# Lower parts of weights and softplus moved from GpSimd to VectorE, and the second layer's state-space parameters issued later, in a two-layer hybrid block

## The chip, the cores and the metric

The kernel runs on one core of a Trainium2 chip. The metric is device time in microseconds of one execution, the median over runs. The engines are called by the names of the profile: PE (TensorE), DVE (VectorE), ACT (ScalarE), POOL (GpSimd), SP (SyncE, which issues the DMAs here).

## What is computed

Two layers, each an RMS norm, an input projection, three mixers side by side, an output projection, and a gated MLP. The sequence is 16 meta tokens and 512 tokens, width 1024, all in float32. Cut to the main lines:

```python
for l in range(2):
    hn = rmsnorm(h, norm1_g[l])
    sq, sk, sv, rq, rk, rv, rg, u = split(hn @ w_in[l])
    sb_o = stick_breaking(rmsnorm(sq), rmsnorm(sk), sv)      # 6 heads of 64
    ro = rmsnorm(retention(rotary(rmsnorm(rq)), rotary(rmsnorm(rk)), rv)) * silu(rg)   # 6 heads
    so = s5_mixer(u, lam, dt, B, C, d, w_glu)                # 16 groups of 16 channels, 64 states each
    h = h + concat(sb_o, ro, so) @ w_out[l]
    hn = rmsnorm(h, norm2_g[l])
    h = h + (silu(hn @ w_gate[l]) * (hn @ w_up[l])) @ w_down[l]
return h[:, 16:]

# stick_breaking, masked to s < t:
z = q @ k.T / 8
between = reverse_cumsum(log_sigmoid(-z)) - log_sigmoid(-z)
w = exp(log_sigmoid(z) + between);  out = w @ v
# s5_mixer, a complex linear recurrence per group g and state p:
x[l] = a * x[l-1] + (f*B) @ u[l];  y = Re(C @ x) + d*u;  y = gelu(y);  return y * sigmoid(y @ w_glu)
```

## The kernel before

Tiles hold 128 features by 528 positions (the 512 tokens of the last layer's end alone). A projection block is 128 output features; for each of 8 slices of the input width it takes three products, since every float32 operand is split into an upper and a lower part: xh by wh, xl by wh, xh by wl. Each product is two matmuls of 264 columns, so a block is 48 matmuls named pj. A weight arrives by DMA as wr, ACT copies it to the upper part wh, and `tensor_tensor` subtracts to give the lower part wl (`Unit.split`). `Unit.lo_eng` says on which engine: for the 23 projection blocks of a layer `WENG = (1, 1, 0)` gives two of three to POOL, of the output projection every second unit goes to POOL, and the MLP's all go to DVE. The attention's softplus is split in the same way: `sb_group` makes sp on DVE, hi on ACT, lo on POOL (`slow_split(s, n, G)`), and matmuls named z then add the running sums with the constant matrices tri and ones. Group widths are 432, 416 and 512 columns; there are 18 such splits in a layer, three head pairs by two heads by three groups.

The parameters of the state-space mixer are made by `s5_params` for each layer: `inputs(ri)` writes four pieces of ws and transposes them on PE (wps), `outputs` makes gg and bbd and multiplies them (kps), `phasors` doubles a table of rotations phr, phi from 1 to 132 columns with many small products (py, st). For the first layer they are shared by DVE and POOL. For the second they all run on POOL, beside the first layer's MLP, spawned at its second block.

The MLP goes through 22 blocks of 128 in parts of 8, 8 and 6. Of each block, gate and up are projected, DVE scales them out of PSUM (ga, up), ACT and DVE make the sigmoid si, POOL multiplies (up), DVE multiplies (ga), ACT makes hi, POOL lo. The eight down projections of a part come behind the gate and up of the next part's first block; they read hi and lo of all eight blocks, the eighth last.

The order of the work is set by a planner in the kernel. Every stage is a generator in `tasks`; between matmuls `tick` lets those go on whose time `t[1]` has come by a clock of estimated durations (`busy["PE"]`, with the costs in the `Timed` tables for V, SC and G). A task's time is raised by `spend` with each instruction and can be raised by hand (`now[0][1] += ...`). Behind it a scheduler of the framework orders the instructions once more, by its own estimates. Each engine then runs its queue strictly in order, so an instruction that stands ahead of its data holds back what is behind it.

Of the kernel before, what the change touches and what calls it, by code (L numbers as in the profile page):

```python
# [15 lines left out]
P = 128  # L16
# [4 lines left out]
KD = DM // P  # L21
DFF = 2816
NF = DFF // P
HALF = T // 2
NT_SLOTS = 62
AHEAD = 4
WLAG = 1000
LEAD = 200
# [4 lines left out]
ZBANKS = 4  # L33
GROUPS = 8
HOLD = (2, 0)
WENG = (1, 1, 0)
EPS = 1e-6
Q = 4
NCH = T // Q
# [46 lines left out]
COL = {"sq": C_SQ, "sk": C_SK, "sv": C_SV, "rq": C_RQ, "rk": C_RK, "rv": C_RV, "rg": C_RG, "u": C_U}  # L86
# [3 lines left out]
def hybrid_kernel(ctx, tc, A, out, dbg=None):  # L90
# [4 lines left out]
    now = [None]  # L95
# [35 lines left out]
    G = Timed(nc.gpsimd, "G", {"one": (180, 2.1), "two": (180, 2.1), "memset": (100, 0.85)})  # L131
# [53 lines left out]
    def banks(n):  # L185
        yield from take(n, "bank")
# [132 lines left out]
    plan, units = [], []  # L319
    for l in range(LAYERS):  # L320
        for i, (n, p) in enumerate(proj_order(l)):
            plan.append((A["w_in"][l, COL[n] // P + p], KD, P, G if plan and WENG[i % len(WENG)] else V))
        for ks in OUT_PARTS[l]:
            for m in range(KD // 2):
                plan.append((A["w_out"][l, m, :, ks[0]:ks[0] + len(ks), :], len(ks), 2 * P, G if m % 2 else V))
        for kind, i, f0, nf in mlp_order():
            if kind == "down":
                plan.append((A["w_down"][l, i, :, f0:f0 + nf, :], nf, P, V))
            else:
                plan.append((A["w_gate" if kind == "gate" else "w_up"][l, i], KD, P, V))  # L330
# [210 lines left out]
    def s5_params(l, engines, scal, par):  # L541
# [44 lines left out]
        def inputs(ri):  # L586

            mul, add, sub = on(engines[ri])
            pr, pi = powers(0, Q)
            x1, x2 = tt("btmp"), tt("btmp")  # L590
            ws = [tt("ws"), tt("ws")]
            for hf in range(2):
                G.memset(ws[hf], 0.0)
            mul(v4(x1, Q), wide(bbi if ri else bbr, Q), pr)
            mul(v4(x2, Q), wide(bbr if ri else bbi, Q), pi)
            yield
            for q in range(2):
                r = slice(64 * q, 64 * q + 64)
                for hf in range(2):
                    o = ws[hf][r, :512].rearrange("p (m c) -> p m c", c=32)[:, :, 16 * q:16 * q + 16]  # L600
                    a, b = (x[r, 256 * hf:256 * hf + 256].rearrange("p (m c) -> p m c", c=16) for x in (x1, x2))
                    (add if ri else sub)(o, a, b)
            yield
            for hf in range(2):
                yield from banks(1)
                ps = bank("wps")
                for t in range(4):
                    TE.transpose(ps[:, P * t:P * t + P], ws[hf][:, P * t:P * t + P], ident)
                yield
                we[ri, hf] = tt("we")  # L610
                SC.copy(out=we[ri, hf][:, :512], in_=ps)
                yield
                freed(1)
            over.append("inputs")

        def outputs():
# [21 lines left out]
            for ri, src in ((0, bbr), (1, bbi)):  # L638
                G.memset(bbd[ri][:, :256], 0.0)
                for q in range(2):  # L640
                    engines[ri].tensor_scalar(
                        out=bbd[ri][64 * q:64 * q + 64, :256].rearrange("p (t c) -> p t c", c=32)[:, :, 16 * q:16 * q + 16],
                        in0=src[64 * q:64 * q + 64], scalar1=-1.0 if ri else 1.0, scalar2=None, op0=ALU.mult)
            now[0][1] += 2000
            yield
            for hf in range(2):
                yield from banks(1)
# [186 lines left out]
    def sb_group(zp, g, gi, place, hl, ws):  # L834


        n = width(g)
        yield
        z = zp[:, :n]
        e = tt("e")  # L840
        SC.activation(e[:, :n], z, AF.Abs)
        SC.activation(e[:, :n], e[:, :n], AF.Exp, scale=-1.0)
        SC.activation(e[:, :n], e[:, :n], AF.Ln, bias=oneb)
        yield
        s = tt("sp")
        V.scalar_tensor_tensor(out=s[:, :n], in0=z, scalar=0.0, in1=e[:, :n], op0=ALU.max, op1=ALU.add)
        yield
        hl[gi] = yield from slow_split(s, n, G)

        for part in range(2):  # L850
            mm(zp[:, :n], lhsT=tri, rhs=hl[gi][part][:, :n], start=False, stop=True, more=True)
        behind = {}
        for j, q0, q1, o0 in g:
            for i, (g1, o1, p0) in place.items():
                if i > j:
                    a = max(q0, p0)
                    behind.setdefault(i, (g1, o1 + a - p0, q1 - a, []))[3].append(o0 + a - q0)
        if any(t[0] not in hl for t in behind.values()):
            yield lambda: all(t[0] in hl for t in behind.values())
        for g1, o1, w, to in behind.values():  # L860
            d, c = zp[:, to[0]:to[0] + w], slice(o1, o1 + w)
            if len(to) == 2:
                f = to[1] - to[0]
                d = zp[:, to[0] + w - f:to[0] + w + f].rearrange("p (t c) -> p t c", t=2)[:, :, f - w:]
            for part in range(2):
                x = hl[g1][part][:, c]
                mm(d, lhsT=ones, rhs=x[:, None, :].to_broadcast([P, 2, w]) if len(to) == 2 else x,
                   start=False, stop=True, more=True)
        yield
        SC.activation(e[:, :n], z, AF.Exp)  # L870
        yield
        freed(1, "scores", "bank")
        ws[gi] = e
# [442 lines left out]
```

## Time and profile before

| | us |
|---|---|
| median of 3 runs | 1374.18 (1373.87 to 1376.58) |
| the profiled execution, its time | 1374.02 |
| its span, first to last instruction | 1372.3 |
| PE busy | 1329.3 (97%) |
| DVE busy | 778.9 (57%) |
| ACT busy | 588.2 (43%) |
| POOL busy | 468.8 (34%) |

By stages: the first layer's projections, mixers and output projection run to about 312 us, its MLP to about 720, the second layer's mixers to about 970, its MLP to the end. A stretch in which PE is busy all the time is limited by the matmuls themselves. Where PE is not, what it waited for is named in the row behind it. The granted clock is that of TensorE as a share of 2.4 GHz.

### The profile page before, as it was taken

The numbers are of one execution on the slowest core, as the hardware profiler recorded it, in microseconds if no ns is written. First come the engines' busy times: TensorE is split into PE (matmuls) and PEld (weight loads), VectorE is DVE, ScalarE is ACT, GpSimd is POOL, SyncE is SP. The second block draws the span as 40 slices with busy tenths as digits, with TensorE's granted clock in tenths as the row PEclk, the third lists the DMA queues.
The fourth block names the chain that finished last, engine by engine and source line by source line (L and its number), as shares of the span: only waits on it lengthen the run. The fifth ranks groups of instructions, "written<-read, shape, count | busy, mean of one in ns | idle before, by whom it ended". The sixth has DMA issues, their size and how long they took to land.

```text
span 1372.3 us, 22298 instructions
## 1 busy us (share of the span) xinstructions
PE 1329.3 (97%) x9068; PEld 1212.8 (88%) x9068; DVE 778.9 (57%) x1261; ACT 588.2 (43%) x937; POOL 468.8 (34%) x598
## 2 busy tenths in 40 slices
PE   7989989999799999999999999999999999999998
PEld 6989879899799999999999899898788888888886
DVE  8874687767436345534567964334575543554453
ACT  5545545555233223322355466564354422332231
POOL 6593553322999012200233532342222210220120
PEclk9999999999999999999999999999999999999999
DMA  5212221222212322222222131312222322233223
GB/s 172 70 47 71 86 79 51 75 85 93 101 53 73 106 78 93 93 93 93 77 93 93 47 102 47 102 55 82 82 100 99 101 92 92 92 99 101 92 80 105
DMA packets 39127, 118.25 MB, mean 86 GB/s; under 512 B 4976, under 2 KB 5488, under 8 KB 39024
## 3 DMA queue, kind: packets, MB, share of 16 engines
q1 hardware_dynamic: 39024, 116.82, 26.0%
q8 instruction: 71, 1.16, 0.3%
q14 instruction: 32, 0.26, 0.1%
HBM read 111.46 MB, written 2.10 MB: 83 GB/s over the span
## 4 chain that ended last, share of the span: by engine, by line
PE 80%; DVE 10%; POOL 6%; ACT 2%; issue 1%; DMA 1%; SPq 0%; DVEq 0%; POOLq 0%
PE pj L138 70%; PE z L138 4%; PE hps L138 2%; PE av L138 1%; DVE fr L125 1%; PE ro L138 1%; DVE ysm L125 1%; DVE wl L125 1%; DVE fi L125 1%; POOL st L125 1%; DVE y L125 1%; POOL py L125 1%; POOL gg L125 1%; DVE s5w L125 1%; POOL ws L125 1%
## 5 line engine op out<-in xcount | busy, mean ns | idle before, releaser
L138 PE MATMUL pj<-xh,wh 128*128 128x264 f32 (+1 forms) x1792 | 448.2, 311 | 8.8 <-ACT wh L125 5.1
L138 PE MATMUL pj<-xh,wl 128*128 128x264 f32 (+1 forms) x1792 | 445.6, 309 | 1.4 <-DVE wl L125 1.4
L138 PE MATMUL pj<-xl,wh 128*128 128x264 f32 (+1 forms) x1792 | 445.1, 310 | 1.1 <-DVE xl L125 1.0
L125 ACT CAST wh<-wr 128x1024 fp32r<-128x1024 f32 (+3 forms) x210 | 206.2, 983 | 404.4 <-PE pj L138 372.4
L138 PEld LDWEIGHTS pj<-xh,wh 128*128 128x128 f32 x1792 | 296.5, 191 | 24.9 <-ACT wh L125 5.1
L138 PEld LDWEIGHTS pj<-xl,wh 128*128 128x128 f32 x1792 | 296.9, 190 | 18.7 <-DVE xl L125 1.6
L138 PEld LDWEIGHTS pj<-xh,wl 128*128 128x128 f32 x1792 | 295.8, 190 | 17.7 <-DVE wl L125 1.6
L125 DVE TENSOR_TENSOR wl<-wr,wh 128x1024 fp32r<-128x1024 f32 (+3 forms) x165 | 243.1, 1474 | 75.7 <-ACT wh L125 75.6
L138 PE MATMUL pj<-lo,wh 128*128 128x264 f32 (+1 forms) x720 | 192.9, 321 | 0.0
L138 PE MATMUL pj<-hi,wh 128*128 128x264 f32 (+1 forms) x720 | 192.2, 322 | 0.0
L138 PE MATMUL pj<-hi,wl 128*128 128x264 f32 (+1 forms) x720 | 191.9, 321 | 0.1
L125 POOL TENSOR_TENSOR up<-ga,up 128x528 f32<-128x528 f32 (+1 forms) x44 | 60.7, 1379 | 350.3 <-DVE up L125 350.3
L125 DVE TENSOR_TENSOR h<-h,pj 128x264 f32<-128x264 f32 (+1 forms) x144 | 69.3, 510 | 136.4 <-PE pj L138 136.1
L125 POOL TENSOR_TENSOR wl<-wr,wh 128x1024 fp32r<-128x1024 f32 (+3 forms) x45 | 95.9, 2133 | 148.2 <-ACT wh L125 126.4
L138 PEld LDWEIGHTS pj<-hi,wl 128*128 128x128 f32 x720 | 119.5, 188 | 10.9 <-DVE wl L125 0.5
L138 PEld LDWEIGHTS pj<-hi,wh 128*128 128x128 f32 x720 | 119.5, 188 | 10.8 <-ACT wh L125 0.6
L138 PEld LDWEIGHTS pj<-lo,wh 128*128 128x128 f32 x720 | 119.7, 188 | 10.0
L125 POOL TENSOR_TENSOR lo<-ga,hi 128x528 fp32r<-128x528 f32 (+1 forms) x44 | 59.0, 1341 | 156.4 <-ACT hi L125 156.3
L125 DVE TENSOR_TENSOR up<-pj,R 128x264 f32<-128x264 f32 (+1 forms) x66 | 32.1, 513 | 97.7 <-PE pj L138 97.7
L125 DVE TENSOR_TENSOR ga<-si,up 128x528 f32<-128x528 f32 (+1 forms) x44 | 31.8, 724 | 81.7 <-ACT si L125 58.4
L125 ACT ACTIVATE si<-si,bias 128x528 f32<-128x528 f32 (+1 forms) x44 | 32.1, 731 | 91.5 <-DVE si L125 91.5
L125 ACT ACTIVATE e<-z 128x432 f32<-128x432 f32 (+2 forms) x72 | 37.7, 547 | 44.7 <-PE z L138 44.3
(220 smaller groups left out, 1510.2 us busy)
## 6 DMA issues: line engine op xcount, KB each, us to landing
wr<-in_w_in_dram SPq DMA_DIRECT2D x44, 512.0 KB, 3.5
wr<-in_w_gate_dram SPq DMA_DIRECT2D x44, 512.0 KB, 3.5
wr<-in_w_up_dram SPq DMA_DIRECT2D x44, 512.0 KB, 3.5
wr<-in_w_down_dram SPq DMA_DIRECT2D x32, 512.0 KB, 3.5
wr<-in_w_out_dram SPq DMA_DIRECT2D x16, 384.0 KB, 3.2
wr<-in_w_down_dram SPq DMA_DIRECT2D x16, 384.0 KB, 3.1
rc<-in_rope_dram SPq DMA_DIRECT2D x12, 264.0 KB, 3.8
rs<-in_rope_dram SPq DMA_DIRECT2D x12, 264.0 KB, 3.9
```

The lines of the kernel that those rows point to most:

```text
L125: return f(*a, **k)
L138: nc.tensor.matmul(out, lhsT=lhsT, rhs=rhs, start=start, stop=stop, skip_group_check=more)
```

## The change

Three edits. The lower parts of all weights and of the attention's softplus are made on DVE (`WENG` is gone, G is V in two rows of the plan, and `slow_split(s, n)` takes its default engine); the split of the small matrix w_glu and the MLP's lo stay on POOL. The second layer's transposes are held back on the planner's clock by 12 us ahead of each half, and the products in `outputs` by 12 us in place of 2; for the first layer both numbers stay, with one more yield. The pool of 528-column tiles has 63 buffers in place of 62.

```diff
-NT_SLOTS = 62
+NT_SLOTS = 63
-WENG = (1, 1, 0)
         for i, (n, p) in enumerate(proj_order(l)):
-            plan.append((A["w_in"][l, COL[n] // P + p], KD, P, G if plan and WENG[i % len(WENG)] else V))
+            plan.append((A["w_in"][l, COL[n] // P + p], KD, P, V))
         for ks in OUT_PARTS[l]:
             for m in range(KD // 2):
-                plan.append((A["w_out"][l, m, :, ks[0]:ks[0] + len(ks), :], len(ks), 2 * P, G if m % 2 else V))
+                plan.append((A["w_out"][l, m, :, ks[0]:ks[0] + len(ks), :], len(ks), 2 * P, V))
...
             for hf in range(2):
+                now[0][1] += 12000 * l
+                yield
                 yield from banks(1)
                 ps = bank("wps")
...
-            now[0][1] += 2000
+            now[0][1] += 2000 + 10000 * l
             yield
...
-        hl[gi] = yield from slow_split(s, n, G)
+        hl[gi] = yield from slow_split(s, n)
```

What this does to the queues, at three places. On PE, in the first layer's MLP, at the end of the fifth block's gate projection (pj); wps are the transposes of the second layer's ws. Before:

```order
L138 MATMUL pj_4468<-xh_3838,wl_4322 128x264
L138 MATMUL pj_4469<-xh_3838,wl_4322 128x264
L144 MATMUL wps_4476<-ident,ws_4200 128x128 x4
L144 MATMUL wps_4504<-ident,ws_4201 128x128 x4
L144 MATMUL wps_4532<-ident,ws_4208 128x128 x4
L138 MATMUL pj_4545<-xh_3621,wh_4381 128x264
L138 MATMUL pj_4546<-xh_3621,wh_4381 128x264
```

And with the change, in the projections behind that place:

```order
L137 MATMUL pj_4613<-xh_3648,wh_4480 128x264
L137 MATMUL pj_4613<-xl_3649,wh_4480 128x264
L143 MATMUL wps_4624<-ident,ws_4200 128x128 x4
L137 MATMUL pj_4613<-xh_3648,wl_4481 128x264
L137 MATMUL pj_4613<-xh_3681,wh_4480 128x264
```

The first four transposes have 65 more pj matmuls ahead of them than before, and the three other groups follow 61, 48 and 26 pj matmuls apart, where three of the four stood together.

On POOL, in the same MLP, around lo of the eighth block (the row with ga and hi), which the first down projection reads; phr, phi, py and st are the phasors of the second layer. Before:

```order
L125 TENSOR_TENSOR phi_4227<-py_4228,py_4229 128x4x64
L125 TENSOR_TENSOR st_4241<-st_4241 128x4
L125 TENSOR_TENSOR phi_4236<-py_4237,py_4238 128x4x64
L125 TENSOR_TENSOR st_4232<-st_4232 128x4 x2
L125 TENSOR_TENSOR st_4241<-st_4241 128x4 x2
L125 TENSOR_TENSOR lo_5148<-ga_5134,hi_5147 128x528
L125 TENSOR_TENSOR py_4228<-phr_4226,st_4232 128x4x4
```

With the change:

```order
L124 TENSOR_TENSOR phi_4227<-py_4228,py_4229 128x4x32
L124 TENSOR_TENSOR st_4241<-st_4241 128x4
L124 TENSOR_TENSOR lo_5111<-ga_5097,hi_5110 128x528
L124 MEMSET tz_5161 128x528
L124 MEMSET tz_5283 128x528
L124 TENSOR_TENSOR phi_4236<-py_4237,py_4238 128x4x32
L124 TENSOR_TENSOR st_4232<-st_4232 128x4 x2
```

The doubling step on 64 columns stood ahead of this lo and now stands behind it, with the clearing of tz.

On DVE, in the first layer's attention, around the first softplus (sp) of the first head pair and the scaling of the second u block; wl are weights' lower parts, phr, phi, py, st the first layer's phasors. Before:

```order
L125 SCALAR_TENSOR_TENSOR sk_648<-sk_648,cols,hsq_763 128x528
L125 TENSOR_TENSOR u_891<-pj_723,R_143 128x264
L125 SCALAR_TENSOR_TENSOR sp_908<-z_753,e_833 128x416
L125 TENSOR_TENSOR u_891<-pj_724,R_143 128x264
L125 SCALAR_TENSOR_TENSOR sp_938<-z_754,e_837 128x416
L125 TENSOR_TENSOR py_803<-phr_801,st_807 128x4
L125 TENSOR_TENSOR py_804<-phi_802,st_807 128x4
L125 TENSOR_TENSOR phr_801<-py_803,py_804 128x4
```

With the change:

```order
L124 SCALAR_TENSOR_TENSOR sp_926<-z_760,e_791 128x416
L124 TENSOR_TENSOR lo_897<-sp_815,hi_896 128x432
L124 TENSOR_TENSOR u_965<-pj_888,R_143 128x264
L124 TENSOR_TENSOR py_851<-phr_849,st_855 128x4
L124 TENSOR_TENSOR u_965<-pj_889,R_143 128x264
L124 TENSOR_TENSOR py_852<-phi_850,st_855 128x4
L124 TENSOR_TENSOR wl_995<-wr_886,wh_994 128x1024
L124 TENSOR_TENSOR phr_849<-py_851,py_852 128x4
L124 TENSOR_TENSOR lo_1023<-sp_877,hi_1022 128x432
```

The lower parts of sp and of a weight now stand between the scaling of u and the phasors, in one queue with them.

## Rows read from the trace of the kernel before

**Rows 1.** The page: busy us (share of span) x instructions.
```profile
PE 1329.3 (97%) x9068; PEld 1212.8 (88%) x9068; DVE 778.9 (57%) x1261; ACT 588.2 (43%) x937; POOL 468.8 (34%) x598
```

**Rows 2.** Stretches: length, busy us by PE, PEld, DVE, ACT, POOL; granted clock, DMA.
```profile
48.00:100.00 52.00, 47.17 (x353) 43.92 (x352) 45.47 (x120) 27.56 (x52) 45.44 (x103) 0.97 0.15 52
140.00:200.00 60.00, 55.39 (x401) 48.98 (x401) 45.98 (x76) 28.76 (x55) 31.87 (x26) 0.97 0.26 85
368.00:383.00 15.00, 5.75 (x28) 5.14 (x28) 4.77 (x7) 3.70 (x5) 14.71 (x24) 0.66 0.10 37
383.00:440.00 57.00, 55.95 (x458) 54.94 (x457) 28.57 (x42) 20.34 (x29) 56.70 (x162) 1.00 0.20 66
440.00:720.00 280.00, 280.00 (x2296) 280.00 (x2296) 137.50 (x186) 94.20 (x121) 51.74 (x47) 1.00 0.28 91
740.00:800.00 60.00, 56.16 (x431) 52.59 (x431) 53.10 (x100) 29.94 (x54) 26.28 (x20) 0.97 0.21 71
```

**Rows 3.** Timeline of PE: start, us, what, xcount [idle before <-releaser].
```profile
368.06 0.40 PE L138 MATMUL pj<-xh,wl 128*128 128x264 f32 x2
376.65 1.97 PE L144 MATMUL wps<-ident,ws 128*128 128x128 f32 x8 [8.19 <-POOL ws L125]
...
380.45 0.79 PE L138 MATMUL pj<-xh,wh 128*128 128x264 f32 x2
...
383.64 0.60 PE L144 MATMUL wps<-ident,ws 128*128 128x128 f32 x4
```

**Rows 4.** Timeline of POOL at the same place.
```profile
373.93 6.39 POOL L125 TENSOR_TENSOR ws<-btmp,btmp 64x256 f32<-64x256 f32 x8
```

**Rows 5.** Who waited for whom, PE: us in total, times, longest.
```profile
PE pj L138 <- DVE u L125: 3.3, 1, 3.3
...
PE z L138 <- POOL lo L125: 1.5, 1, 1.5
...
PE kps L138 <- POOL bbd L125: 1.0, 2, 0.8
```

**Rows 6.** Groups by form: xcount | busy us, mean ns | idle before; the last from 460:480.
```profile
L125 POOL TENSOR_TENSOR wl<-wr,wh 128x1024 fp32r<-128x1024 f32 x30 | 72.5, 2419 | 96.6 <-ACT wh L125 91.6 <-ACT e L125 4.9
...
L125 POOL TENSOR_TENSOR lo<-sp,hi 128x512 fp32r<-128x512 f32 x12 | 17.6, 1480 | 19.7 <-ACT hi L125 11.0 <-issue 8.7
...
L125 DVE TENSOR_TENSOR wl<-wr,wh 128x1024 fp32r<-128x1024 f32 x3 | 3.7, 1225 | 0.6 <-ACT wh L125 0.6
```

**Rows 7.** Timelines of POOL and DVE, 24 to 32 and 68 to 74 us.
```profile
25.43 5.08 POOL L125 TENSOR_TENSOR wl<-wr,wh 128x1024 fp32r<-128x1024 f32 x2 [1.06 <-ACT wh L125]
...
28.30 2.33 DVE L125 TENSOR_TENSOR s5w<-s5p 128x16 f32<-128x16 f32 x2
...
30.76 0.70 DVE L125 TENSOR_TENSOR lo<-acc,hi 128x528 fp32r<-128x528 f32 x1
31.38 0.25 DVE L125 TENSOR_TENSOR s5w<-s5p 128x16 f32<-128x16 f32 x2
...
69.53 2.40 POOL L125 TENSOR_TENSOR wl<-wr,wh 128x1024 fp32r<-128x1024 f32 x1
...
69.71 2.24 DVE L125 TENSOR_TENSOR phr<-py,py 128x4 f32<-128x4 f32 x1
...
73.85 0.20 DVE L125 TENSOR_TENSOR phr<-py,py 128x8 f32<-128x8 f32 x1
```

**Rows 8.** POOL's busy us in the three dense stretches: tile wl, then tile sp.
```profile
sum 172.00, POOL 25.85; mean POOL 8.62
...
sum 172.00, POOL 15.79; mean POOL 5.26
```

**Rows 9.** POOL's and PE's timelines at the first down projection; a phasor group.
```profile
440.19 1.34 POOL L125 TENSOR_TENSOR lo<-ga,hi 128x528 fp32r<-128x528 f32 x1
...
445.16 0.40 PE L138 MATMUL pj<-hi,wh 128*128 128x264 f32 x2
...
L125 POOL TENSOR_TENSOR py<-phr,st 128x256 f32<-128x256 f32 x4 | 2.4, 611 | 0.0
```

## The prediction

> **What bounds the kernel now.** I read the page's share of busy time first, then the stretches, then the timeline where TensorE (PE) falls short. PE is busy 97% of the span [rows 1]. In the MLP of the first layer, from 440 to 720 us, it has no idle time at all: 2296 matmuls in 280 us, 0.122 us each, while VectorE (DVE) is busy half of the time and GpSimd (POOL) a fifth [rows 2]. Nothing done on DVE or POOL shortens such a stretch. Time can be won only where PE waits, and three kinds of places stand out: one hole at 368 to 383 us, where PE works 5.75 of 15 us at a mean granted clock of 0.66; and the attention stages of both layers, where PE loses a few us in each of the dense stretches 48 to 100, 140 to 200 and 740 to 800 us [rows 2]. In these three DVE is busy 45.5 of 52, 46.0 of 60 and 53.1 of 60 us, so it is the engine that PE comes to wait for there. The profiled execution took 1374.02 us (span 1372.3 and 1.7 around it); the median of the runs is 1374.18, so I sum against 1374.0 and take the result as the median's. A measurement of this kernel tells about 0.2% (2.7 us) from no change; "same" below means 1371.4 to 1376.9.
>
> **The change, part 1: the second layer's parameters are held back in the issue order.** In the kernel before, three rows of four transposes each (wps) stand in PE's queue directly behind the gate projection of the fifth MLP block. PE gets to them at 368.3 us and waits 8.19 us for POOL to write ws [rows 3]; POOL writes the eight pieces of ws in a row from 373.93 us on, 0.80 us each [rows 4]. PE does the queue in order, so ready matmuls stand behind. After the idle time PE is on the lower of its two clocks, 1.2 GHz: the first pair of pj matmuls takes 0.79 us in place of 0.41, and the mean of 0.66 in rows 2 says that the low level held for some 10 of the 15 us. The price: from 368.3 to 383.64 us, 15.3 us, PE does 12 transposes and 17 pj matmuls (nine rows, from the one at 380.45 on). At the pace of rows 2, 17 x 0.122 = 2.1 us; the transposes are at most 0.60 us for four, so 1.8 us, and less since such rows overlap the next. The loss is 15.3 - 2.1 - 1.8 = 11.4 us at least, about 12.0 with the overlap.
>
> In the new order the first four transposes stand 65 pj matmuls later, the next 61, 48 and 26 after that. At 0.122 us, PE gets to the first at 368.3 + 7.9 = 376.2 us, counted on the old clock of events. POOL's rows up to ws are the same in both orders, and POOL does not wait for PE there, so the third piece, the last one that the first transposes read, is there at 373.93 + 3 x 0.80 = 376.3. What is left of the wait is 0 to 0.5 us; the other three groups stand 3 us or more behind their data. **Minus 12.0 us**, and the half clock goes with it. Next late behind it are the kps matmuls, which wait 1.0 us for POOL's bbd [rows 5]. The change holds them back too (82 and 106 pj matmuls further), and in POOL's order bbd has moved ahead: **minus 1.0**. The new yield ahead of each transpose group and the added issue times are zero for the first layer; there only the planner's order moves.
>
> **Part 2: 81 lower parts go from POOL to DVE.** These are 45 of weights (30 with 1024 columns) and 36 of the attention's softplus (432, 416 and 512 columns). On POOL a weight's lower part takes 2419 ns, an attention one of 512 columns 1480; on DVE with POOL idle a weight's takes 1225 ns, and the same subtraction on 528 columns 0.70 us [rows 6, 7]. So DVE pays 0.51 of POOL's time for the one and about 0.46 for the other, an estimated 70 us in all (30 x 1.225 = 37; 15 smaller weights at about 0.8; 36 at 0.58 to 0.68), on a queue that lies beside PE's.
>
> What that costs or gives is not in those durations alone, and this is the unknown of the case. While POOL does a lower part, DVE's own instructions stretch. From 25.43 to 30.5 us POOL does two weights; in that time two DVE instructions on 16 columns take 2.33 us, and two of the same kind right after it 0.25. At 69.53 POOL starts another, of 2.40 us; DVE's phr<-py,py on 4 columns takes 2.24 us beside it, and 0.20 on twice the columns when POOL does short work [rows 7]. So DVE lost over 2 us to each, and would itself have needed 1.23. The Trainium skill ("SBUF — State Buffer", Who interferes with whom) states why: a DVE instruction with two SBUF inputs and a GpSimd instruction that reads SBUF hold a shared pair of ports for the whole instruction, and the second one blocks. The trace agrees at these places. Taken for every moved instruction, that rule would give back all of POOL's time below and make the time 1374.0 - 13.0 - 41.6 + 20.4 = 1339 at best.
>
> Two of PE's waits stem from this: the 3.3 us for u, whose read of PSUM stands behind that phr on DVE, and the 1.5 us for lo, which stands behind that weight on POOL [rows 5]. With POOL's part gone both causes are gone: **minus 4.8**, at most.
>
> Against it stands the longer DVE queue in the three dense stretches. The moved instructions fill 25.85 (weights) and 15.79 us (attention) of POOL's time there [rows 8]. On DVE they cost 25.85 x 0.51 + 15.79 x 0.46 = 20.4 us. What comes back is between nothing and all 41.6 us. The two places of rows 7 would give back over 80%, but both are instructions with two operands in SBUF, many of DVE's in the attention read PSUM (sp<-z, u<-pj), and where DVE waits for input nothing comes back; I take 40%, 16.6 us. The DVE queue is then 3.8 us longer in these stretches, and I charge it all to PE: **plus 3.8**. The ends are +20.4 and -21.2. Outside them I count nothing: DVE has idle time there, and from 440 to 720 us, where it is busy half of the time, PE never waits. [...]
>
> **Other moved work.** NT_SLOTS 63 adds one buffer to a pool of 62; I find no wait that names a missing tile, so nothing. The planner, given other costs, issues the attention's steps later against the pj matmuls (the last scores of the first layer's third pair stand behind its last projection, with no pj among them); part of the +3.8 is for that. The second layer's MLP stands in the same order in both.
>
> Sum: 1374.0 - 12.0 - 1.0 - 4.8 + 3.8 = **1360 us**.
>
> **Rivals.** *First, the attention wins more* (the blocked time comes back nearly whole): with 80%, 33.3 us, DVE's queue is 12.9 us shorter in the dense stretches. PE can win no more than it idles there, 4.8 + 4.6 + 3.8 = 13.2 us by rows 2, and 4.8 of it is counted. With half of the other 8.4: 1360 - 3.8 - 4.2 = 1352, down to 1348 with all of it. For it: rows 7. Against it: much of PE's waiting there is for chains (ScalarE's hsq, a rotation's DMA), not for DVE's load.
>
> *Second, DVE is a partial bound*: nothing comes back where it matters in one layer, half of the 20.4 is paid: 1360 - 3.8 + 10.2 = 1366, up to 1371. For it: DVE is 77 to 88% busy in those stretches.
>
> *Third, the hole moves.* POOL is busy 56.7 of 57 us from 383 to 440 [rows 2], with work that does not wait for PE, so without the hole PE comes 13 us earlier to whatever POOL makes. The first down projection reads the eighth block's lo 0.73 x 7 us after its start, at 445.16; POOL writes it from 440.19 to 441.5 [rows 9]. Had lo kept its place, PE would wait 441.5 - (445.2 - 13.0) = 9.3 us, and the time would be 1369. In the new order the whole last doubling of the phasors is behind lo: eight products of 0.61 us, 4.9 us, and an estimated 11 with their sums, the small steps between and the clearing of tz. So it lands at about 430.5, before 432.2; if only the 4.9 were saved it would come at 436.6 and PE would wait 4.4: 1364.
>
> *Fourth, slower than before*: DVE becomes what ends last in the dense stretches and gives nothing back; then PE pays the 20.4 whole and keeps the waits of 4.8: 1360 + 4.8 - 3.8 + 20.4 = 1381. It is slower than the bound if less than 4.5 of the 41.6 us comes back (20.4 - 4.5 = 15.9 against a gain of 13.0 plus 2.7). Rows 7 alone show more than 4 us of it.
>
> *Fifth, the change doesn't do what it says*: held back on the planner's clock, the transposes could still come before ws on the chip. The counts above say 0 to 0.5 us; if ws came 8 us later than I count, the first group would wait as before: about 1372.
>
> **How the numbers follow.** Forecast 1360 (1356 to 1364): 0.50. First rival 0.17, second 0.18, third 0.06, fourth 0.05, fifth 0.04. The range 1351 to 1370 takes in the forecast, most of the first rival, the second but for its end and the third: about 0.82. Faster (under 1371.4): 0.50 + 0.17 + 0.16 + 0.05 = 0.88; same: 0.02 + 0.01 + 0.04 = 0.07; slower: 0.05.
>
> **What would show it.** Part 1 is right if PE's wait for ws is under 1 us, the clock from 360 to 400 us is at 1.00 throughout, and the stretch between the two layers' attention is 13 us shorter. Part 2: POOL's busy time falls by some 140 us (both groups of rows 6 gone), DVE's rises by less than the 70 us that it pays; the difference is what came back. PE's waits for u (3.3) and for lo (1.5) should be gone; more waits for DVE in 140 to 200 us would be the second rival, a wait of the first down projection for lo the third. Wrong it would be if PE's idle time in the first 310 us grew by more than 13 us.

## The result, and the profile after

The changed kernel takes 1346.03 us (1345.35 to 1346.87), beside 1374.03 us (1373.74 to 1376.58) for the kernel before on the same chip: a ratio of 0.9787, with a 95% interval of 0.9775 to 0.9799. That is 28 us faster where I had forecast 14, and it lies below my range of 1351 to 1370. The profiled execution took 1346.14 us, its span is 1344.4. Of the run e7_none below, one of four executions took 3238 us at a granted clock of 0.40; its figures are those of the other three.

The busy times of the changed kernel, in the form of [rows 1]:

```profile
PE 1316.5 (98%) x9068; PEld 1203.5 (90%) x9068; DVE 800.6 (60%) x1342; ACT 586.8 (44%) x937; POOL 341.6 (25%) x517
```

POOL has lost 127 us, DVE has gained 22: the 81 moved instructions cost DVE some 70, so about 48 came back to it. On this my forecast was close. (The 81 took 142 us on POOL; the rest of POOL's work has grown by about 15, and why is not shown.) The same stretches as in [rows 2], of the changed kernel (length; busy us of PE, PEld, DVE, ACT, POOL; granted clock; DMA):

```profile
48.00:100.00 52.00, 51.49 (x414) 48.89 (x413) 48.80 (x136) 30.78 (x57) 47.85 (x115) 1.00 0.19 65
140.00:200.00 60.00, 56.21 (x439) 52.51 (x438) 48.68 (x89) 27.07 (x50) 18.62 (x18) 0.97 0.29 90
368.00:383.00 15.00, 13.99 (x114) 13.58 (x113) 8.02 (x13) 6.16 (x10) 14.92 (x45) 1.00 0.19 63
383.00:440.00 57.00, 57.00 (x468) 56.31 (x467) 29.32 (x44) 19.86 (x27) 55.60 (x140) 1.00 0.30 92
740.00:800.00 60.00, 58.45 (x463) 54.48 (x462) 50.54 (x87) 35.75 (x64) 9.60 (x7) 1.00 0.28 94
```

In two of the three dense stretches DVE is busier than before (48.8 against 45.5, 48.7 against 46.0), in the third less (50.5 against 53.1): 3.4 us more in all, near the 3.8 of my forecast. PE nevertheless does more in each: 414 matmuls against 353, 439 against 401, 463 against 431.

Stretches at fixed times hold different work in the two kernels. Two places can be found in every kernel of this case: the first matmul of the first layer's second norm (tile nps; the first layer's mixers and output projection are then done, and the first projections of the MLP, which do not need the norm yet, too, so this is later than the 312 us named above), and the same of the second layer's first norm (the first MLP is done). Cut there, each of the three stages holds the same work in both kernels: 2347 matmuls in the first, give or take one, 3175 in the second, 3552 in the third. The kernel before:

```profile
0.00:326.80 326.80, 304.30 (x2347) 283.61 (x2348) 239.66 (x524) 173.39 (x318) 158.02 (x231) 0.98 0.25 82
326.80:727.20 400.40, 390.10 (x3175) 388.48 (x3174) 195.12 (x266) 136.80 (x180) 152.17 (x257) 0.99 0.27 88
727.20:1372.00 644.80, 634.86 (x3552) 540.68 (x3550) 344.08 (x471) 278.04 (x441) 158.66 (x110) 1.00 0.27 87
```

and the changed one:

```profile
0.00:314.00 314.00, 296.53 (x2346) 279.34 (x2347) 246.85 (x565) 172.73 (x317) 98.46 (x190) 0.99 0.27 86
314.00:703.90 389.90, 387.46 (x3174) 386.18 (x3173) 193.79 (x268) 136.23 (x179) 150.64 (x255) 1.00 0.28 91
703.90:1344.00 640.10, 632.53 (x3552) 537.96 (x3550) 359.99 (x510) 277.86 (x441) 92.46 (x72) 1.00 0.27 88
```

So the 28 us are 12.8 in the first layer's mixers, 10.5 in its MLP and 4.6 behind it (645.1 to 640.5 up to the end of the spans). I had forecast 13 for the MLP and 1 for all the rest. In the first stage DVE is busy 7.2 us longer, and the stage is 12.8 us shorter. Of these 12.8 us, PE's idle time makes 5.0 (22.5 to 17.5) and its busy time 7.8 (304.3 to 296.5, for the same matmuls). The length of DVE's queue, by which I had priced it, points the wrong way.

### The profile page after: what moved, and what is told of

It is laid out like the page before. It is cut to its first block, busy times and chain, and to the rows that moved or that the text cites. A ratio compares the mean times of both kernels' runs of the same rounds, so it can differ in the third digit from the quotient of the medians.

```text
span 1344.4 us, 22300 instructions
## 1 busy us (share of the span) xinstructions
PE 1316.5 (98%) x9068; PEld 1203.5 (90%) x9068; DVE 800.6 (60%) x1342; ACT 586.8 (44%) x937; POOL 341.6 (25%) x517
## 4 chain that ended last, share of the span: by engine, by line
PE 87%; DVE 6%; POOL 3%; ACT 2%; issue 1%; DMA 1%; SPq 0%; DVEq 0%; POOLq 0%; ACTq 0%
PE pj L137 75%; PE z L137 4%; PE hps L137 2%; PE av L137 1%; PE ro L137 1%; DVE wl L124 1%; ACT e L124 1%; DVE ysm L124 1%; POOL gg L124 1%; PE kps L137 1%; POOL ws L124 1%; PE rtp L143 0%; ACT uc L124 0%; POOL btmp L124 0%; PE kv L137 0%
## 5 line engine op out<-in xcount | busy, mean ns | idle before, releaser
L137 PE MATMUL pj<-xh,wh 128*128 128x264 f32 (+1 forms) x1792 | 454.4, 310 | 15.2 <-ACT wh L124 4.9
L137 PE MATMUL pj<-xl,wh 128*128 128x264 f32 (+1 forms) x1792 | 454.8, 310 | 1.2 <-DVE xl L124 1.2
L137 PE MATMUL pj<-xh,wl 128*128 128x264 f32 (+1 forms) x1792 | 452.4, 309 | 0.3 <-DVE wl L124 0.3
L124 DVE TENSOR_TENSOR wl<-wr,wh 128x1024 fp32r<-128x1024 f32 (+3 forms) x210 | 292.9, 1395 | 84.9 <-ACT wh L124 82.1
L137 PEld LDWEIGHTS pj<-lo,wh 128*128 128x128 f32 x720 | 119.9, 188 | 10.1
L124 ACT CAST hi<-ga 128x528 fp32r<-128x528 f32 (+1 forms) x44 | 27.6, 627 | 62.2 <-DVE ga L124 62.2
```

The lines of the kernel that those rows point to most:

```text
L124: return f(*a, **k)
L137: nc.tensor.matmul(out, lhsT=lhsT, rhs=rhs, start=start, stop=stop, skip_group_check=more)
```

## Experiments

Three questions: is the MLP's gain that of the holds; is the mixers' gain that of the engine (DVE no longer blocked, lower parts no longer late) or that of the planner's new order; and what does a us of work on DVE cost PE, against a us in which POOL blocks DVE? The stage times (the same cuts, from the trace of one execution of each run; the last to the end of the span) and the ratios, which are over all executions:

| kernel | lower parts made on | plan | holds | mixers 1 | MLP 1 | the rest | ratio to before (95%) |
|---|---|---|---|---|---|---|---|
| before | POOL | POOL's costs | no | 326.8 | 400.4 | 645.1 | 1 |
| changed | DVE | DVE's costs | yes | 314.0 | 389.9 | 640.5 | 0.979 (0.978 to 0.980) |
| e1_holds | POOL | POOL's | yes | 330.0 | 388.9 | 652.8 | 0.997 (0.996 to 0.998) |
| e2_engines | DVE | DVE's | no | 315.3 | 400.2 | 639.8 | 0.986 (0.984 to 0.988) |
| e5_plan | POOL | DVE's | yes | 324.1 | 389.4 | 641.7 | 0.987 (0.985 to 0.988) |
| e6_queue | DVE | POOL's | yes | 315.1 | 389.1 | 646.6 | 0.983 (0.982 to 0.985) |
| e7_none | nobody | POOL's | yes | 304.7 | 394.0 | 640.7 | 0.974 (0.972 to 0.975) |
| e8_unread | POOL, not read | POOL's | yes | 325.6 | 389.0 | 645.4 | 0.991 (0.989 to 0.993) |
| e3_sp_pool | softplus's on POOL | DVE's | yes | 316.7 | 389.5 | 645.8 | 0.983 (0.982 to 0.985) |
| e4_wl_pool | weights' on POOL | DVE's | yes | 321.0 | 389.2 | 643.9 | 0.986 (0.985 to 0.988) |
| e9_yield | POOL | POOL's | yield only | 329.2 | 398.3 | 649.5 | 1.005 (1.003 to 1.007) |
| e11_lead | DVE | DVE's, LEAD 220 | yes | 312.9 | 390.2 | 642.7 | 0.981 (0.979 to 0.984) |
| e12_lead_before | POOL | POOL's, LEAD 220 | no | 324.6 | 398.9 | 646.4 | 0.997 (0.996 to 0.998) |
| e10_more | DVE, and 18 more | DVE's | yes | 319.9 | 389.5 | 641.3 | 0.983 (0.981 to 0.986) |

The profiled execution need not be the median one: of e9_yield it took 1378.8 us and the median is 1382.1, of e11_lead 1347.5 and 1349.3. So differences of a few us between single stages are to be read with care. The kernels whose lower parts POOL makes by POOL's plan, and the two that leave them out, have 62 of the 528-column buffers, all others 63; this third edit was not varied by itself.

### One part alone

The kernel before with the holds:

```diff
+                now[0][1] += 12000 * l
+                yield
                 yield from banks(1)
                 ps = bank("wps")
...
-            now[0][1] += 2000
+            now[0][1] += 2000 + 10000 * l
```

> The kernel before with part 1 alone: the second layer's transposes and the products of outputs are held back by 12 and 10 us, all lower parts stay on POOL. My forecast gave this part -13.0 us of its sum, so 1361 us, with the hole at 368 to 383 us gone. If the parts add up and the attention is where the rest of the gain lies, the change's total of 28 us leaves 15 to 20 us for part 2, so part 1 alone is 1361 to 1364 us. If the hole is not the holds' doing (rival: POOL, freed of the weights' lower parts, is simply earlier with ws), part 1 alone gives less than 6 us: 1368 us or more.

It took 1372.28 us, where the kernel before took 1375.94 on that chip: 0.3% faster. By its time that is the rival's range (1368 or more), but the stages tell otherwise. The MLP is 11.5 us shorter, as my forecast has it, while the first layer's mixers are 3.2 us longer and the rest 7.7. So the holds close the hole by themselves, with POOL as busy as before, and most of the gain is lost elsewhere; what takes it is the question of e9_yield below.

The other part alone is the changed kernel with both edits of the diff above undone:

> The changed kernel without the holds: the 81 lower parts are on DVE, the second layer's transposes stand where the planner then puts them. By my forecast's sum part 2 alone is worth -1 us: 1373. If the parts add up with what was measured for both (1346) and part 1 is worth 10 to 13, it is 1356 to 1359 us. If POOL's relief alone closes the hole, it is 1350 us or less.

It took 1357.2 us, a gain of 1.4% and as expected if the parts add up (1356 to 1359), and the MLP is as long as before (400.2). PE waits there for POOL just as in [rows 3]; of what PE waited for (us in total, times, longest):

```profile
PE wps L143 <- POOL ws L124: 9.3, 2, 8.2
```

So POOL's relief does not close the hole, the holds do, and part 2 is worth 18.7 us alone, where my sum had 1. On the changed kernel the holds are worth 10.3 us in the MLP and about the same in the time (the ratios are 0.9861 and 0.9787, which is 10.2 us), since the mixers lose nothing there.

### Engine or order

The planner decides the order by the costs of the engine that it is told. So the two can be taken apart: `X` is issued on one engine and spends the other's costs.

```diff
+    X = Timed(nc.gpsimd, "V", {"one": (150, 1.05), "two": (160, 1.2)})
...
-            plan.append((A["w_in"][l, COL[n] // P + p], KD, P, V))
+            plan.append((A["w_in"][l, COL[n] // P + p], KD, P, X if plan and WENG[i % len(WENG)] else V))
...
-        hl[gi] = yield from slow_split(s, n)
+        hl[gi] = yield from slow_split(s, n, X)
```

> The changed kernel's plan with the engine of before: the planner is told DVE's costs for the 81 lower parts, so that PE's order is nearly that of the changed kernel, but the instructions are issued on POOL. Theory A (the gain in the attention is the new order of the work): it keeps most of the attention's gain, 1346 to 1351 us. Theory B (the gain is that DVE and the chains behind the lower parts no longer stand behind POOL's slow instructions): most of that gain goes, 1357 us or more, and worse than that where the plan now expects a lower part earlier than POOL has it.

The mirror image starts from the kernel before with the holds, with `X = Timed(nc.vector, "G", {"one": (180, 2.1), "two": (180, 2.1)})` in G's place.

> The other way round, holds included: the planner is told POOL's costs for the 81 lower parts, so that PE's order is nearly that of the kernel before with the holds alone, but the instructions are issued on DVE. Theory A (order): little of the attention's gain is left, 1356 to 1361 us. Theory B (blocked DVE instructions and slow chains): most of it is there, 1346 to 1351 us. If DVE's longer queue cost what my forecast charged (3.8 us) and only the waits for u and lo went, 1359 to 1361 us.

They took 1357.8 us (theory B) and 1353.1 us (between the two), and the stages sort it. In the first layer's mixers the engine counts: 330.0 to 315.1 in the old order, 324.1 to 314.0 in the new one, while the order makes 5.9 with POOL and 1.1 with DVE. Behind the MLP it looks like the order: 652.8 to 641.7 and 646.6 to 640.5, while the engine makes 6.2 in the old order and 1.2 in the new one. The first pair differs in the number of buffers too; the second (both 63) does not, and gives the engine 10.1 us in the mixers. The orders of a pair are near each other but not the same. Written by name and shape in the order of the trace, PE's 9,068 matmuls of e5_plan differ from the changed kernel's in 402 lines, from those of the kernel before in 2,278; those of e6_queue differ from e1_holds in 452.

### What blocking costs, and what the work costs

These two leave the lower parts out of the result. In the first nobody makes them, in the second POOL makes them and no matmul reads them; in both the matmuls read zeros in their place, as many as before.

```diff
+            if self.lo_eng is X:
+                b = zero[:, None, :self.c].to_broadcast([P, self.kt, self.c])
...
-        return R_(a), R_(b)
+        return R_(a), zero if lo_eng is X else R_(b)
```

> The kernel before with the holds, planned with POOL's costs, but the 81 lower parts are left out on every engine: nobody makes them, and the matmuls that would read them read a tile of zeros (the same number of matmuls; the lower parts' share of the result is missing). It shows what these lower parts cost in all where POOL does them, and, against the same plan with them on DVE (1353 us), what DVE's longer queue costs PE. By my forecast's sum DVE's 20.4 us in the dense stretches are paid by PE: 1353 - 20 = 1333 us. If DVE's queue is not what PE pays for: 1349 to 1353 us.

> As the run that leaves the lower parts out, and with PE's order the same as there, but POOL makes all 81 lower parts as before, into tiles that no matmul reads (the matmuls read zeros, so the lower parts' share of the result is missing). POOL's work is there, and nobody waits for its results. Theory B1 (POOL's instructions block DVE's): it is 10 to 18 us slower than the run without them, so 1360 us or more. Theory B2 (PE waits for lower parts that are late on POOL): it is within 3 us of that run, and the whole difference to the holds alone (1372) is PE's waiting.

They took 1338.3 us, between the two values given for it, and 1362.25 us: 24.0 us apart (20.6 between the profiled executions), with PE's order the same but for 26 lines. No matmul waits for what POOL makes in the second, so the difference is what POOL's presence does to others. That is theory B1, and more than its 10 to 18 us. What is left to the holds alone (ratios 0.9911 and 0.9969, 8 us) is what waiting for late lower parts can have cost at most, as far as the two can be compared: their orders differ in 942 lines, and PE's list of waits there has 1.5 us for a lower part on POOL. The groups of DVE's instructions show how POOL acts on them. With nobody making the lower parts (xcount | busy us, mean ns | idle before):

```profile
L125 DVE TENSOR_TENSOR wl<-wr,wh 128x1024 fp32r<-128x1024 f32 (+3 forms) x165 | 250.0, 1516 | 75.9 <-ACT wh L125 75.6
...
L125 DVE TENSOR_TENSOR h<-h,pj 128x264 f32<-128x264 f32 (+1 forms) x144 | 69.5, 510 | 137.9 <-PE pj L143 137.5
...
L125 DVE SCALAR_TENSOR_TENSOR sp<-z,e 128x432 f32<-128x432 f32 (+2 forms) x36 | 21.9, 622 | 18.4 <-ACT e L125 14.6 <-PE pj L143 3.8
...
L125 DVE COPY uc<-u 32x132 f32<-32x132 f32 x32 | 8.9, 278 | 0.5
...
L125 DVE SCALAR_TENSOR_TENSOR sq<-sq,cols,hsq 128x528 f32<-128x528 f32 x6 | 5.5, 924 | 4.2 <-ACT hsq L125 4.2
...
L125 DVE SCALAR_TENSOR_TENSOR rk<-rk,cols,hsq 128x528 f32<-128x528 f32 x6 | 4.7, 780 | 5.4 <-ACT hsq L125 5.4
...
L125 DVE TENSOR_SCALAR s5w<-s5w 128x16 f32<-128x16 f32 x13 | 2.4, 215 | 0.0
```

and with POOL making them unread:

```profile
L125 DVE TENSOR_TENSOR wl<-wr,wh 128x1024 fp32r<-128x1024 f32 (+3 forms) x165 | 245.7, 1489 | 73.9 <-ACT wh L125 73.8
...
L125 DVE TENSOR_TENSOR h<-h,pj 128x264 f32<-128x264 f32 (+1 forms) x144 | 69.6, 510 | 138.1 <-PE pj L139 137.7
...
L125 DVE SCALAR_TENSOR_TENSOR sp<-z,e 128x432 f32<-128x432 f32 (+2 forms) x36 | 21.8, 622 | 16.3 <-ACT e L125 12.4 <-PE pj L139 3.8
...
L125 DVE COPY uc<-u 32x132 f32<-32x132 f32 x32 | 11.0, 343 | 0.5
...
L125 DVE SCALAR_TENSOR_TENSOR rk<-rk,cols,hsq 128x528 f32<-128x528 f32 x6 | 8.8, 1473 | 5.0 <-ACT hsq L125 4.9
L125 DVE SCALAR_TENSOR_TENSOR sq<-sq,cols,hsq 128x528 f32<-128x528 f32 x6 | 8.6, 1425 | 8.6 <-ACT hsq L125 8.6
...
L125 DVE TENSOR_SCALAR s5w<-s5w 128x16 f32<-128x16 f32 x13 | 4.7, 385 | 0.0
```

What has an operand in PSUM beside one in SBUF (h, whose pj is in PSUM; sp, whose z is) takes the same 510 and 622 ns. Several groups of the mixers that read two operands in SBUF take longer beside POOL, such as rk with 1473 ns in place of 780 and sq with 1425 in place of 924. Not every such group does: DVE's own wl, most of it in the MLPs, where POOL does the same work in both runs, takes 1489 and 1516 ns. Two kinds with one operand in SBUF take longer too, the COPY (343, 278) and the TENSOR_SCALAR (385, 215). In each of these it is one instruction, held behind a weight on POOL; for the COPY (two of them in the first row, one of the usual length):

```profile
724.62 2.64 DVE L125 COPY uc<-u 32x132 f32<-32x132 f32 x2
...
724.74 2.39 POOL L125 TENSOR_TENSOR wl<-wr,wh 128x1024 fp32r<-128x1024 f32 x1 [6.57 <-ACT wh L125]
```

All of DVE's work is 779.3 us against 737.3, the same 1262 instructions; ACT's is 587.5 us in both, and PE's commonest matmul (pj with xh and wh) takes 311 ns against 309 in the mean.

One place shows how that reaches PE. With POOL at work, DVE (above), POOL and PE (the last row), start and us:

```profile
68.94 2.26 DVE L125 TENSOR_TENSOR phr<-py,py 128x4 f32<-128x4 f32 x1
71.23 1.03 DVE L125 TENSOR_TENSOR py<-phr,st 128x4 f32<-128x4 f32 x1
...
74.70 2.32 DVE L125 TENSOR_TENSOR py<-phi,st 128x16 f32<-128x16 f32 x1
...
77.89 0.43 DVE L125 TENSOR_TENSOR u<-pj,R 128x264 f32<-128x264 f32 x1
...
68.77 2.41 POOL L125 TENSOR_TENSOR wl<-wr,wh 128x1024 fp32r<-128x1024 f32 x1
71.13 1.11 POOL L125 TENSOR_TENSOR lo<-sp,hi 128x432 fp32r<-128x432 f32 x1
...
74.65 2.34 POOL L125 TENSOR_TENSOR wl<-wr,wh 128x1024 fp32r<-128x1024 f32 x1
...
78.37 0.59 PE L139 MATMUL pj<-xh,wh 128*128 128x264 f32 x1 [6.86 <-DVE u L125]
```

and the same DVE instructions where POOL doesn't make them:

```profile
63.12 0.17 DVE L125 TENSOR_TENSOR phr<-py,py 128x4 f32<-128x4 f32 x1
63.33 0.17 DVE L125 TENSOR_TENSOR py<-phr,st 128x4 f32<-128x4 f32 x1
...
65.92 0.20 DVE L125 TENSOR_TENSOR py<-phi,st 128x16 f32<-128x16 f32 x1
...
67.08 0.42 DVE L125 TENSOR_TENSOR u<-pj,R 128x264 f32<-128x264 f32 x1
```

Three instructions on 4 to 16 columns take 5.6 us in place of 0.5, and each ends within 0.03 us of POOL's instruction beside it (71.20 and 71.18, 72.26 and 72.24, 77.02 and 76.99). Behind them stands the reading of u out of PSUM, 9.0 us after the first of them in place of 4.0, and behind that PE, which waits 6.86 us.

Now the two prices. The first stage of three kernels in the old order: nobody, POOL unread, DVE (e6_queue).

```profile
0.00:304.70 304.70, 295.30 (x2346) 278.75 (x2347) 212.29 (x525) 173.72 (x317) 92.15 (x191) 1.00 0.28 88
```

```profile
0.00:325.60 325.60, 301.82 (x2347) 283.53 (x2348) 238.88 (x525) 173.77 (x318) 158.60 (x232) 0.98 0.26 83
```

```profile
0.00:315.10 315.10, 299.36 (x2346) 279.74 (x2347) 248.45 (x565) 174.13 (x317) 95.62 (x190) 1.00 0.27 86
```

With POOL at work DVE is busy 26.6 us longer by blocking alone (40% of POOL's 66.5), and the stage is 20.9 us longer: 0.79 us for each us. With the work on DVE it is busy 36.2 us longer, and the stage 10.4: 0.29 for each. Behind the MLP there is no such difference in the old order: POOL costs 4.7 us, DVE 5.9. All in all POOL's presence costs 24.0 us for 42.0 us more of DVE's busy time (0.57 for each), DVE's work 13.5 (by the ratios, 0.9736 and 0.9834) for 67.6 more (804.9 against 737.3; 0.20 for each). Three things blur the figures of DVE's work: e6_queue's order differs from the other two in some 930 lines, it has one buffer more, and without any lower parts the MLP is 5 us longer, 2.9 of them one wait for a weight's lower part at 420 us.

### Which of the lower parts

The changed kernel and its plan, with only the softplus's or only the weights' lower parts issued on POOL, by the same `X`:

> The changed kernel with its plan (DVE's costs for all 81), but the 36 lower parts of the softplus are issued on POOL; the weights' stay on DVE. With all 81 on POOL in this plan it was 1357.8, so there are some 12 us to divide. If POOL blocks DVE in proportion to its time, the softplus has 47 of 143 us: 1350 us. If what counts is that the matmuls behind the softplus wait longer for its lower part, most of the 12 us is here: 1354 us or more.

> The changed kernel with its plan, but the 45 weights' lower parts are issued on POOL as in the kernel before; the softplus's stay on DVE. In proportion to POOL's time (96 of 143 us) it loses 8 of the 12 us: 1354 us. If the matmuls behind the softplus are what counts: 1346 to 1349 us.

They took 1352.89 and 1356.51 us. In the first layer's mixers the softplus costs 2.7 us there, the weights 7.0, all together 10.1 (e5_plan): a sum of 9.7, in the shares 28 and 72%, close to the 33 and 67% of POOL's time. No sign, then, that the matmuls behind the softplus count for more. In the whole time neither meets its proportion (1350 and 1354): the two add to 17 us and both at once cost 11.8; the difference lies behind the MLP (645.8 and 643.9 against 641.7), where I can't tell it from reordering.

### How much a reordering makes

> The kernel before with only the added yield ahead of each transpose group (no hold, all lower parts on POOL). With the holds alone the stretch of the first layer's MLP became 11.5 us shorter, but the time fell by less than 4: the first layer's mixers ended 3 us later and the second layer's took 4 us more. If the yield's reordering of the first layer's mixers is what took the 3 us: the first layer's mixers end at 329 to 331 us here too (327 in the kernel before) and the time is 1376 to 1380. If the loss belongs to the holds, which act in the second layer only, the mixers end as before and the time is 1374 to 1376.

The yield alone took 1382.12 us, 0.5% slower, a little above the 1376 to 1380 that I gave for its theory. The first layer's mixers end at 329.2 us, as with the holds (330.0). PE's waits show the same new places in both, such as 5.1 us for u where it was 3.3 in [rows 5] and 3.7 for y that the kernel before didn't have:

```profile
PE pj L138 <- DVE u L125: 5.1, 1, 5.1
PE pj L138 <- DVE y L125: 3.7, 1, 3.7
```

So the yield, which does nothing but reorder, explains the 3 us in the mixers, and 4.4 of the 7.7 us behind the MLP; the other 3.3 are not explained.

> The changed kernel with one number of the planner moved a little (LEAD 220 in place of 200), which changes the order of the mixers' work and nothing else. It measures how much of a difference a mere reordering makes on the changed kernel. If the order of the mixers is a matter of luck of several us, the time is anywhere from 1342 to 1352; if the changed kernel's mixers no longer depend on it, since DVE is not blocked, within 2 us of 1346.

> The same small move of the planner's number on the kernel before, with POOL making the lower parts. If the mixers with POOL in them are sensitive to their order, the time moves by 3 us or more either way (1368 to 1380); if not, within 2 us of the kernel before.

LEAD is a constant of the planner. At 220 it gave 1349.3 us on the changed kernel and 1371.51 on the kernel before (0.9972, 2.9 us faster, between the two answers given). The first is not clear of the changed kernel's own ratio (0.979 to 0.984 against 0.978 to 0.980) and decides nothing; its stages moved by -1.1, 0.3 and 2.2 us. In the kernel before the three stages moved by -2.2, -1.5 and 1.3. A number that moves no work between engines thus makes 1 to 2 us in a stage, and the yield 2 to 4. Beside that scatter the first layer's mixers stand clear: six kernels with all the lower parts on POOL end them at 324.1 to 330.0 us, four with them on DVE at 312.9 to 315.3 (the run below, with 18 more instructions moved, at 319.9). Behind the MLP the two sets overlap, 641.7 to 652.8 and 639.8 to 646.6. So the engine's share in the mixers is shown, and what the order makes is not told apart from chance: neither its 5.9 us in the mixers with POOL nor the 4.6 behind the MLP.

### Carried on

```diff
-        G.tensor_tensor(out=m1, in0=t, in1=c, op=ALU.mult)
+        V.tensor_tensor(out=m1, in0=t, in1=c, op=ALU.mult)
...
-        G.tensor_tensor(out=s, in0=s, in1=rg, op=ALU.mult)
+        V.tensor_tensor(out=s, in0=s, in1=rg, op=ALU.mult)
```

> The changed kernel carried on: the first product of the rotations (12 of 528 columns, 1.4 us each on POOL) and the product with the gate (6 of 528, 1.3 us) go from POOL to DVE too. By the rates that the runs so far give (a us in which POOL blocks DVE costs PE about 0.54 us, a us of DVE's own work 0.20), 25 us on POOL block DVE by 0.30 x 25 = 7.5 us, worth 4.0, and cost DVE an estimated 13 us, worth 2.6: 1.4 us faster, 1344 to 1346, if the reordering doesn't weigh more. If the DVE queue has become the bound in the changed kernel, slower: 1350 or more.

It took 1351.96 us (0.9834 of the kernel before): a miss, some 6 us slower than the changed kernel and in the range given for DVE's queue as the bound (1350 or more). The MLP and the rest are as long as there within 1 us, the first layer's mixers are 5.9 us longer. Most of the loss shows in one place; the stretches (columns as in [rows 2]) of this kernel

```profile
220.00:240.00 20.00, 14.19 (x88) 11.68 (x86) 19.12 (x46) 13.73 (x28) 1.21 (x2) 0.84 0.00 0
240.00:260.00 20.00, 20.00 (x132) 16.00 (x132) 8.04 (x14) 9.78 (x22) 2.15 (x1) 0.73 0.00 1
```

and of the changed one

```profile
220.00:240.00 20.00, 18.87 (x163) 16.18 (x164) 17.75 (x38) 9.54 (x18) 5.00 (x6) 1.00 0.41 120
240.00:260.00 20.00, 20.00 (x171) 18.73 (x168) 13.91 (x31) 14.23 (x29) 4.14 (x4) 1.00 0.12 36
```

From 222 to 256 us PE has only the scores, sums and outputs of the mixers before it, no projection, where the changed kernel does 79 matmuls of the output projection between them. PE waits for lo, e, ysm and sc, 1.0 to 1.8 us each (all but e come from DVE), DVE is busy 19 of the first 20 us, and the mean clock falls to 0.84 and 0.73. My rates priced the moved work and not the place to which the planner moved the rest. No run that computes the whole result beats the changed kernel.

## Why the prediction was wrong

The direction and the split into two parts were right, the size of part 2 was not. Step by step:

**The hole: right, mis-sized.** Minus 13.0 with the kps was forecast, 11.5 (alone) and 10.3 (on the changed kernel) were measured. The first transposes come at 365.10 us without a wait and kps at 403.97 without one, so they do come after ws and bbd; the fifth rival is out. Of the changed kernel's PE, around the first:

```profile
361.11 0.41 PE L137 MATMUL pj<-xh,wl 128*128 128x264 f32 x2
362.95 0.36 PE L137 MATMUL pj<-xh,wh 128*128 128x264 f32 x1 [1.43 <-DVE ga L124]
...
365.10 0.60 PE L143 MATMUL wps<-ident,ws 128*128 128x128 f32 x4
...
403.97 1.94 PE L137 MATMUL kps<-gg,bbd 128*32 128x128 f32 x16
```

What I had not named as late next is in the second row, and with two more like it makes 2.5 us:

```profile
PE pj L137 <- DVE ga L124: 2.1, 2, 1.4
...
PE wps L143 <- DVE ga L124: 0.4, 1, 0.4
```

It is not new work. POOL's up, queued behind the products for ws, starts at 359.89; DVE's ga<-si,up waits for it, and behind that on DVE stand the scalings that free PSUM for the next projection:

```profile
361.25 1.21 DVE L124 TENSOR_TENSOR ga<-si,up 128x528 f32<-128x528 f32 x1 [3.50 <-POOL up L124]
362.38 0.76 DVE L124 TENSOR_TENSOR ga<-pj,R 128x264 f32<-128x264 f32 x2
```

In the kernel before the same chain ran at 374 us, under the hole. The hole did not move to the first down projection: from 383 to 440 us PE has no idle time.

**The waits for u and lo (minus 4.8): gone, as forecast.** PE's wait for u is 0.5 us in the changed kernel, and no wait for POOL is left among PE's waits. The new order has its part in it: with the lower parts on DVE in the old order (e6_queue) PE waits 3.2 us for lo, then from DVE, and 1.3 for u.

**The longer DVE queue (plus 3.8): the step that failed.** Its parts were about right: 36.2 us more work on DVE in the first stage where I would have put about half of POOL's 66.5, 40% of POOL's time back. The sum of the two was then charged to PE at one rate, and that is wrong. Blocked time costs PE 0.79 us for each us in the first layer's mixers, DVE's own added work 0.29. By these runs moving the work makes -20.9 + 10.4 = -10.5 in the first stage alone, PE's wait for u included, where my sum had -4.8 + 3.8 = -1.0 for the attention of both layers; the change as a whole made -12.8 there. Why the rates differ the place at 69 to 78 us suggests: a block falls on whatever instruction stands there, a short one in a chain on which PE waits included, while a lower part of a weight is made well ahead of its use. That this is the whole reason was not tested by itself. The Trainium skill ("SBUF — State Buffer", Who interferes with whom) gives the rule for who blocks: DVE instructions with two SBUF inputs, and copies and tensor_scalar in their fast modes. The groups above agree, the COPY and the TENSOR_SCALAR included, which I had left out of account; in which mode these two ran no row shows. (The 1339 us that I worked out beside this rule are 1339.8 by their own terms.)

**The cap of 13.2 us on the attention's gain was too low**, and the first rival (1352, down to 1348) with it: the first layer's mixers and what lies behind the MLP gained 12.8 + 4.6 = 17.4 us. I had counted PE's idle time in three stretches, as if time in which PE is busy could not be won. [Rows 2] also show a granted clock of 0.97 in each, which I priced only in the hole: 0.03 x 172 us is 5.2 us more, in which PE counts as busy. And the 7.8 us of busy time that the first stage lost are more than the clock can have given back there, an estimated 1.7 us (the trace has 10.2 us of the stage at the lower level before and 6.8 in the changed kernel, each at half the pace). What the other 6 us are no row shows; gaps between matmuls that are shorter than a matmul's own record would count as busy.

Over the span the mean clock is 0.991 in the kernel before and 0.997 in the changed one, 12.4 and 4.0 us of lost clock. But in the hole PE mostly idles while the clock is low (columns as in [rows 2], the kernel before):

```profile
372.50:382.70 10.20, 4.98 (x22) 4.59 (x23) 3.55 (x6) 2.65 (x4) 9.91 (x20) 0.50 0.07 27
```

So half of these 5.1 us are idle time already, and the clock makes about 6 of the 28. Between the run with POOL unread (0.992) and the one without the lower parts (0.999) PE's busy time differs by 7.1 us (1324.1 and 1317.0), so at most 7 of the 20.6 us between their spans are the clock, and 13.5 are idle time.

**Behind the MLP (counted at nothing)** 4.6 us were won. By e5_plan and e6_queue this is more the plan's doing than the engine's, but it lies within what reordering alone makes; its cause stays open.

**The other rivals.** With DVE as a partial or whole bound, PE would have paid the work and got little back. By the runs in the old order it paid about 13.5 us and got 24.0 back, so neither came. The third rival did not come either: the hole did not move.

## What to carry to other kernels

Price the blocked time and the added work of an engine apart: what blocks can hit a short instruction on which the matmuls wait, while work that is due later fits where there is room (argued from one place here, not tested by itself). Do not take PE's idle time for all that can be won: in the first stage PE's idle time fell by 5.0 us and its busy time by 7.8 with the same matmuls, and the granted clock accounts for only a part of the latter. Where a planner sets the order, measure a change of its numbers alone first: here an added yield alone cost 0.5%, while the holds and the yield together gained 0.3%.

## What the runs showed of the hardware

At the places shown, a DVE instruction that reads SBUF beside a POOL `tensor_tensor` is not slowed in proportion but held until the other ends: 2.26 and 2.32 us for 4 and 16 columns, beside 2.41 and 2.34 us on POOL, and 0.17 to 0.20 us otherwise. I had expected that of two operands in SBUF, and found it for COPY and TENSOR_SCALAR too (278 to 343 ns and 215 to 385 ns in the mean), not for those that read one operand from PSUM (510 and 622 ns in both runs). The price in the time was 24.0 us for 140 us of POOL's work whose results nobody read.
